# Latent attention: the low-rank rows of the first two pairs of query tiles are loaded ahead of the loads of w_out

## The chip, the cores and the metric

The kernel runs on one core of a Trainium2 chip. The metric is the device time of one launch in microseconds (us); times before are the median of three runs. One further execution was recorded by the hardware profiler, and all rows of the profile come from that one.

## The reference, cut to what matters

Two layers of a hybrid block over 1024 tokens with 1024 features. Each layer has a mixer (differential attention, latent attention and a state-space model side by side, concatenated and multiplied by `w_out`) and a squared-ReLU MLP. The part that the change touches is latent attention:

```python
def _mla(cq, ckv, kr, cos, sin, q_norm_g, w_uq, kv_norm_g, w_ukv):
    q = (_rmsnorm(cq, q_norm_g) @ w_uq).reshape(b, s, MLA_HEADS, MLA_NOPE + MLA_ROPE)
    qn = q[..., :MLA_NOPE]
    qr = _apply_rope(q[..., MLA_NOPE:], cos[:, :, None, :], sin[:, :, None, :])
    kv = (_rmsnorm(ckv, kv_norm_g) @ w_ukv).reshape(b, s, MLA_HEADS, MLA_NOPE + MLA_V)
    kn, v = kv[..., :MLA_NOPE], kv[..., MLA_NOPE:]
    kr = _apply_rope(kr, cos, sin)
    ...
        sc = (jnp.einsum('bqhd,bkhd->bhqk', qnb, kn)
              + jnp.einsum('bqhr,bkr->bhqk', qrb, kr)).astype(jnp.float32) * scale
        p = _masked_softmax(sc, _chunk_mask(start, s))
        return jnp.einsum('bhqk,bkhe->bqhe', p.astype(v.dtype), v)
```

`cq` (256 features) and `ckv` (128 features) are the low-rank rows: 384 floats for each token, projected from the layer's input. The mask lets a query see keys up to the end of its own chunk of 64 tokens, so query tile t needs the keys of tiles 0 to t.

## The kernel before

The 1024 tokens are 8 tiles of 128 (t = 0 to 7). Large products are done as three float32r products each (`mm3`, L191 to L193), from operands split into a high and a low part. The splitting costs a copy on ScalarE (ACT) and a subtraction on VectorE (DVE) for each operand. All DMAs are issued by SyncE (SP), whose queue is in order.

A layer's mixer is written as Python generators that emit instructions and are interleaved by `weave` (L1410): each stream has a weight, and the stream with the smallest progress emits next. The generators fix the source order; the framework's scheduler then fixes the order on each engine when the program is built, and it may put an instruction ahead of one that stands earlier in the source.

The streams that meet around the change, in `mixer`:

- `in_proj` (L749) projects the layer's input. It writes the low-rank rows and the rope part of the keys to a DRAM tensor `d_c` (L827, L828), and at its end runs the state-space model, tile by tile (`ssm`, L1173; its products are L1260, L1271 and L1282, its result is stored at L1289). At the mark "hidden" the last tile of it is still to come.
- `attention` (L1003) is the differential attention; each of its four heads ends with a store of its output into `d_cc` (L997).
- `mla` (L1099) is the latent attention. `lora` (L1019) loads its weights and returns three steps for a tile t. `first(t)` loads 384 floats for each token from `d_c` (L1046), scales them by the two root-mean-square factors (L1047, L1048, DVE), transposes them (L1051, PE) and copies them out (L1054, ACT). `second(t)` multiplies by `w_uq` (L1061) and `w_ukv` (L1063) and applies the rope. `third(t)` transposes queries and keys for all heads (L1090) and splits them (L1094, L1095).
- `load_wout` (L1294) loads eight tiles of `w_out` of 512 KB each (L1298) and splits them (L1302 and L1303, or L1305 on ACT and L1306 on DVE), for the out-projection (`out_proj`, L1311).

In `mla` the local function `ahead(n, i)` does the steps for query pair i, that is tiles 2i and 2i + 1. Pair 0 is done before the mark "hidden" (L1139 to L1142). Pair i + 1 is done between the heads of pair i (L1165): `first` of its first tile after head 0, `first` of its second tile and `second` of its first after head 1, `second` of its second after head 2. Pair i + 1 then begins with `third` (L1146) of both its tiles.

Three weaves follow one another (L1374 to L1378). The second ends when `attention` is done and `in_proj` and `mla` have both reached "hidden". The third weaves the rest of `in_proj`, query pair 0 of `mla`, and `load_wout`; so the loads of tiles 2 and 3 stand between those of `w_out` in the source. After it come the out-projection of tiles 0 and 1 beside query pair 1, and so on.

Buffers come from an arena of 17,856 words for each partition (`Arena`, L44). `get` takes, among the free places that fit, the one whose words were released longest ago; `put` releases. A load into a place must wait until whatever read or wrote the words before is done. Lookups for blocks of 256 words or more go in steps of 256 words.

Of the kernel before, what the change touches and what calls it, by code (L numbers as in the profile page):

```python
# [17 lines left out]
P = 128  # L18
# [12 lines left out]
WOW = 16  # L31
GROUPS = [2] + [4] * 6 + [2, 4]
LEAD = 6
C_Q, C_K, C_V, C_CQ, C_CKV, C_KR, C_Z, C_XBC, C_DT = 0, 256, 512, 768, 1024, 1152, 1184, 1696, 2464

SLOT = 2048
# [70 lines left out]
class Net:  # L107
# [125 lines left out]
    def mlp_up(self, l, hT, bg, late):  # L233
# [27 lines left out]
        N = FF // (2 * P)  # L261
        todo = [(i, True, False) for i in range(LEAD)] + [(i, i >= LEAD, True) for i in range(N)]
        staged = []
# [32 lines left out]
        stage()  # L296
        parts = self.chain(*(forms() for _ in range(LEAD + N)))
        queue = [next(parts) for _ in range(3)]
# [720 lines left out]
    def lora(self, l, st):  # L1019

        nc, F, I = self.nc, self.F, self.i
        p = st["p"]
        wuq, wukv = F.get(2, 384, top=True), F.get(512, top=True)
        nc.sync.dma_start(wuq, I["w_uq"][l].rearrange("(k p) n -> p k n", p=P))
        nc.sync.dma_start(wukv, I["w_ukv"][l])
        for k in range(2):
            nc.scalar.activation(wuq[:, k], wuq[:, k], AF.Copy, scale=p["uq"][k])
        nc.scalar.activation(wukv, wukv, AF.Copy, scale=p["ukv"])
        css = st["css"]
        nc.vector.tensor_add(css[:, 0], css[:, 0], css[:, 1])  # L1030
        rq = self.rsqrt(css[:, 0], 8, 1.0 / 256, RMS_EPS)
        rkv = self.rsqrt(css[:, 2], 8, 1.0 / 128, RMS_EPS)

        kr = F.get(8, 32, top=True)
        tmp = F.get(8, 32)
        k0 = F.get(8, 32)
        nc.sync.dma_start(k0, self.d_c[l].rearrange("(t p) c -> p t c", p=P)[:, :, 384:416])
        nc.vector.tensor_mul(kr.rearrange("p t (a f) -> p t a f", a=2), k0.rearrange("p t (a f) -> p t a f", a=2), self.rcos)
        for a in range(2):
            nc.vector.tensor_mul(tmp[:, :, a * 16:a * 16 + 16], k0[:, :, 16 - a * 16:32 - a * 16], self.rsin[:, :, a, :])  # L1040
        nc.vector.tensor_add(kr, kr, tmp)
        F.put(tmp, k0)

        def first(t):
            cn = F.get(384)
            nc.sync.dma_start(cn, self.d_c[l][t * P:t * P + P, 0:384])  # L1046
            nc.vector.tensor_scalar(cn[:, 0:256], cn[:, 0:256], rq[:, t:t + 1], None, op0=ALU.mult)  # L1047
            nc.vector.tensor_scalar(cn[:, 256:384], cn[:, 256:384], rkv[:, t:t + 1], None, op0=ALU.mult)  # L1048
            ps = self.bank("t")[:, 0:384]
            for k in range(3):  # L1050
                nc.tensor.transpose(ps[:, k * P:k * P + P], cn[:, k * P:k * P + P], self.ident)  # L1051
            F.put(cn)
            cT = F.get(384)
            nc.scalar.copy(cT, ps)  # L1054
            return cT

        def second(t, cT):
            pq = self.bank()[:, 0:384]
            for k in range(2):
                s = slice(k * P, k * P + P)  # L1060
                nc.tensor.matmul(pq, cT[:, s], wuq[:, k], start=k == 0, stop=k == 1)  # L1061
            pk = self.bank()
            nc.tensor.matmul(pk, cT[:, 256:384], wukv, start=True, stop=True)  # L1063
            F.put(cT)
            q = F.get(4, 96)
            pqv = pq.rearrange("p (h e) -> p h e", e=96)
            nc.vector.tensor_copy(q[:, :, 0:64], pqv[:, :, 0:64])
            tq = F.get(4, 32)
            cb = self.rcos[:, t].rearrange("p a f -> p (a f)").unsqueeze(1).to_broadcast([P, 4, 32])
            nc.vector.tensor_mul(q[:, :, 64:96], pqv[:, :, 64:96], cb)  # L1070
            for a in range(2):
                nc.vector.tensor_mul(tq[:, :, a * 16:a * 16 + 16], pqv[:, :, 80 - a * 16:96 - a * 16],
                                     self.rsin[:, t, a].unsqueeze(1).to_broadcast([P, 4, 16]))
            nc.gpsimd.tensor_add(q[:, :, 64:96], q[:, :, 64:96], tq)
            F.put(tq)
            kt = F.get(4, 96)
            pkv = pk.rearrange("p (h e) -> p h e", e=128)
            nc.scalar.copy(kt[:, :, 0:64], pkv[:, :, 0:64])
            nc.gpsimd.tensor_copy(kt[:, :, 64:96], kr[:, t].unsqueeze(1).to_broadcast([P, 4, 32]))
            assert st["heads"] >= (2 if t < 4 else 4)  # L1080
            nc.scalar.copy(st["vml"][:, t], pkv[:, :, 64:128])
            return q, kt

        def third(t, qk):
            tok = slice(t * P, t * P + P)
            dsts = st["QT"][t // 2 % 2][:, :, :, t % 2 * P:t % 2 * P + P], st["KT"][:, :, :, tok]
            pt = self.bank2()
            for n, src in enumerate(qk):
                for h in range(4):
                    nc.tensor.transpose(pt[0:96, (n * 4 + h) * P:(n * 4 + h + 1) * P], src[:, h], self.ident)  # L1090
                F.put(src)
            for n, dst in enumerate(dsts):
                pv = pt[0:96, n * 512:n * 512 + 512].rearrange("p (h q) -> p h q", q=P)
                nc.scalar.copy(dst[0:96, :, 0], pv)  # L1094
                nc.vector.tensor_sub(dst[0:96, :, 1], pv, f32(dst[0:96, :, 0]))  # L1095

        return first, second, third, lambda: F.put(kr, wuq, wukv)

    def mla(self, l, st, cc):  # L1099

        nc, F = self.nc, self.F
        first, second, third, done = self.lora(l, st)
        a, b = {}, {}

        def scores(h, i, pt):
            QT, KT = st["QT"][i % 2][:, h], st["KT"][:, h]
            ll, rl = self.sm(2, "ml_l"), self.sm(2, "ml_rl")
            for tt in range(2):
                n = P * (2 * i + tt + 1)
                tok = slice(tt * P, tt * P + P)  # L1110
                S = self.bank2()
                for c0 in range(0, n, 512):
                    c1 = min(n, c0 + 512)
                    self.mm3(S[:, c0:c1], QT[0:96, 0, tok], QT[0:96, 1, tok],
                             KT[0:96, 0, c0:c1], KT[0:96, 1, c0:c1], True, c1 < n)
                nc.tensor.matmul(S[:, n - 64:n], self.chunk[0:96, 0:P], self.chunk[0:96, P:192], start=False, stop=True)  # L1116
                p = F.get(n)
                self.softmax(S, n, p, self.sm(1, "nm"), ll[:, tt:tt + 1])
                pt.append(p)
                yield  # L1120
            nc.vector.reciprocal(rl, ll)
            pt.append(rl)

        def values(h, i, pt):
            rl = pt.pop()
            yield from self.p_times_v(pt[0], pt[1], i, st["vml"][:, :, h], rl, cc[i][:, :, 256 + h * 64:320 + h * 64])
            F.put(*pt)

        def ahead(n, i):
            t = 2 * i  # L1130
            if n == 0:
                a[t] = first(t)
            elif n == 1:
                a[t + 1] = first(t + 1)
                b[t] = second(t, a.pop(t))
            elif n == 2:
                b[t + 1] = second(t + 1, a.pop(t + 1))

        for n in range(3):  # L1139
            ahead(n, 0)  # L1140
            yield 2.0
        yield "hidden"  # L1142
        held, last = iter(()), None
        for i in range(4):
            for t in (2 * i, 2 * i + 1):
                third(t, b.pop(t))  # L1146
                yield 2.0
                next(held, None)
            cc[i] = F.get(2, D, top=True)
            rows = self.d_cc[l][i * 256:i * 256 + 256].rearrange("(t p) e -> p t e", p=P)  # L1150
            nc.sync.dma_start(cc[i][:, :, 0:256], rows[:, :, 0:256])
            nc.sync.dma_start(cc[i][:, :, 512:1024], rows[:, :, 512:1024])
            for h in range(4):
                pt = []
                for _ in scores(h, i, pt):
                    yield 2.0 + 2 * i
                    next(held, None)
                for _ in held:
                    yield 1.0
                if last is not None:  # L1160
                    yield last
                    last = None
                held = values(h, i, pt)
                if i < 3:
                    ahead(h, i + 1)  # L1165
            last = i
        done()
        for _ in held:
            yield 1.0
        yield last  # L1170
# [436 lines left out]
```

## Time and profile before

| what | us |
|---|---|
| median of 3 runs | 2797.93 |
| lowest and highest of the 3 | 2793.36, 2808.04 |
| the profiled execution's own time | 2798.41 |
| its span, from the first to the last instruction | 2796.6 |
| PE busy in the span | 2621.3 |
| DVE busy | 1749.1 |
| ACT busy | 1110.3 |
| POOL busy | 583.9 |

Times in the profile are counted from the start of the span. PE is TensorE, PEld its weight loads, POOL is GpSimd; a "q" behind an engine (SPq) is its sequencer, and the issue of a DMA is listed there with the time that the issue took, not the transfer. A row of a timeline has start, length, engine, source line, operation, what it writes and reads, and a count; in brackets stand the idle time of the engine before it and what ended that. Latent attention begins at about 447 us in layer 0 and 1810 us in layer 1; the out-projections begin at about 545 and 1896 us.

### The profile page before, as it was taken

Reading aid. Unit: us, or ns where it says so; the run is one execution under the profiler, and the core shown is the slowest. Engines: PE = TensorE matmul, PEld = TensorE weight load, DVE = VectorE, ACT = ScalarE, POOL = GpSimd, SP = SyncE. Lnnn points to the kernel's source line nnn. Section 1 sums busy time; section 2 is a strip of 40 time slices with the busy share of each in tenths; the row PEclk is TensorE's granted clock in tenths of the full one; section 3 lists DMA queues with packets and bytes.
Section 4 is the critical chain, followed back from the end, with each engine's and each line's share of the span. In section 5 each row is a group of like instructions: output and inputs, shape, how many; then the busy total and the mean of one; then the engine's idle time right before and its main releaser. Section 6 shows DMA issues by size and latency. Waiting matters only on the chain.

```text
span 2796.6 us, 34697 instructions
## 1 busy us (share of the span) xinstructions
PE 2621.3 (94%) x12530; PEld 2049.1 (73%) x12530; DVE 1749.1 (63%) x3223; ACT 1110.3 (40%) x2145; POOL 583.9 (21%) x517
## 2 busy tenths in 40 slices
PE   5799999799889999999999998989988999999998
PEld 3677776577667777777778776767766888788886
DVE  7767666544888877666585676664458645543435
ACT  5333334444544446121143434454454555521212
POOL 1341233310244230000021113341014422000002
PEclk9899979899999999999999998989999999999999
DMA  6441312321455557444331131132134432531313
GB/s 228 109 138 55 99 39 75 111 67 53 134 172 168 161 160 242 147 131 140 98 119 49 57 100 60 51 118 72 52 121 136 136 108 103 185 131 61 121 49 102
DMA packets 268527, 311.54 MB, mean 111 GB/s; under 512 B 28674, under 2 KB 212164, under 8 KB 268356
## 3 DMA queue, kind: packets, MB, share of 16 engines
q1 hardware_dynamic: 268356, 309.32, 34.5%
q8 instruction: 99, 1.62, 0.2%
q14 instruction: 72, 0.59, 0.1%
HBM read 242.85 MB, written 66.43 MB: 111 GB/s over the span
## 4 chain that ended last, share of the span: by engine, by line
PE 59%; DVE 5%; DMA 2%; ACT 2%; issue 1%; POOL 1%; DVEq 0%; SPq 0%; ACTq 0%; POOLq 0%
PE bank_b L191 9%; PE bank_b L193 9%; PE bank_b L192 9%; PE bank_s L191 8%; PE bank_s L192 8%; PE bank_s L193 8%; PE bank_s L967 1%; PE bank_a L914 1%; DVE split L231 1%; PE bank_t L927 1%; DVE arena_f L639 1%; PE bank_t L581 1%; PE bank_b L1260 1%; ACT split L230 0%; PE bank_a L943 0%
## 5 line engine op out<-in xcount | busy, mean ns | idle before, releaser
L191 PE MATMUL bank_b<-split 128*128 128x512 f32 (+2 forms) x1824 | 722.1, 396 | 30.5 <-DVE arena_f L217 11.5
L193 PE MATMUL bank_b<-split 128*128 128x512 f32 (+2 forms) x1824 | 702.9, 386 | 2.1 <-DVE split L231 1.3
L192 PE MATMUL bank_b<-split 128*128 128x512 f32 (+2 forms) x1824 | 702.4, 385 | 0.0
L230 ACT CAST split<-arena_f 128x512 fp32r<-128x512 f32 (+1 forms) x424 | 305.1, 749 | 701.4 <-PE bank_s L192 454.3
L191 PE MATMUL bank_s<-split 128*128 128x512 f32 (+2 forms) x1152 | 454.4, 397 | 24.8 <-ACT arena_f L902 6.9
L192 PE MATMUL bank_s<-split 128*128 128x512 f32 (+2 forms) x1152 | 450.9, 391 | 2.3 <-DVE split L231 1.8
L193 PE MATMUL bank_s<-split 128*128 128x512 f32 (+2 forms) x1152 | 448.3, 389 | 0.0
L231 DVE TENSOR_TENSOR split<-arena_f,split 128x512 fp32r<-128x512 f32 (+1 forms) x424 | 386.6, 931 | 94.6 <-ACT split L230 94.3
L191 PEld LDWEIGHTS bank_b<-split 128*128 128x128 f32 x1824 | 349.8, 192 | 108.7 <-ACT split L230 19.5
L193 PEld LDWEIGHTS bank_b<-split 128*128 128x128 f32 x1824 | 348.5, 191 | 69.5 <-issue 3.9
L192 PEld LDWEIGHTS bank_b<-split 128*128 128x128 f32 x1824 | 349.5, 192 | 64.3 <-issue 4.6
L408 DVE TENSOR_TENSOR arena_f<-arena_f,bank_s 128x1024 f32<-128x1024 f32 x126 | 153.6, 1219 | 241.3 <-PE bank_s L193 241.1
L191 PEld LDWEIGHTS bank_s<-split 128*128 128x128 f32 (+1 forms) x1152 | 218.0, 190 | 81.8 <-ACT arena_f L902 10.1
L192 PEld LDWEIGHTS bank_s<-split 128*128 128x128 f32 (+1 forms) x1152 | 219.2, 190 | 48.4 <-DVE split L231 3.5
L193 PEld LDWEIGHTS bank_s<-split 128*128 128x128 f32 (+1 forms) x1152 | 219.0, 190 | 44.6 <-issue 0.8
L901 DVE TENSOR_REDUCE nm<-bank_s 128x1 f32<-128x128 f32 (+3 forms) x192 | 141.0, 752 | 123.0 <-PE bank_s L1116 72.6
L902 ACT ACTIVATE arena_f<-bank_s,nm 128x128 f32<-128x128 f32 (+4 forms) x192 | 142.1, 742 | 163.6 <-DVE nm L901 119.7
L570 DVE SCALAR_TENSOR_TENSOR arena_f<-arena_f,cond 128x128 f32<-128x128 f32 x448 | 162.0, 388 | 46.4 <-DMA arena_f<-in_b_ada 20.4
L696 POOL TENSOR_TENSOR arena_f<-arena_f 128x1024 f32<-128x1024 f32 x14 | 33.6, 2400 | 462.2 <-ACT rstd_y L182 347.6
L930 ACT COPY arena_f<-bank_t 128x512 f32<-128x512 f32 (+1 forms) x160 | 86.9, 543 | 100.6 <-PE bank_t L927 93.4
L246 ACT ACTIVATE arena_f<-arena_f 128x512 f32<-128x512 f32 x128 | 81.0, 633 | 109.9 <-DVE arena_f L331 51.3
L967 PE MATMUL bank_s<-split 32*128 32x512 f32 (+3 forms) x576 | 117.1, 386 | 7.4 <-ACT arena_f L902 5.1
(281 smaller groups left out, 3189.5 us busy)
## 6 DMA issues: line engine op xcount, KB each, us to landing
arena_f<-in_w_ada SPq DMA_DIRECT2D x80, 512.0 KB
d_r<-arena_f SPq DMA_DIRECT2D x128, 256.0 KB
arena_f<-in_w_up SPq DMA_DIRECT2D x32, 1024.0 KB
arena_f<-d_r SPq DMA_DIRECT2D x64, 512.0 KB
arena_f<-in_w_down SPq DMA_DIRECT2D x64, 512.0 KB
arena_f<-d_x SPq DMA_DIRECT2D x36, 512.0 KB
d_x<-arena_f SPq DMA_DIRECT2D x23, 512.0 KB
arena_f<-in_w_in SPq DMA_DIRECT2D x20, 512.0 KB
```

The lines of the kernel that those rows point to most:

```text
L191: mm(out, wh, xh, start=start, stop=False)
L192: mm(out, wh, xl, start=False, stop=False)
L193: mm(out, wl, xh, start=False, stop=stop)
L230: self.nc.scalar.copy(hi, src)
L231: (eng or self.nc.vector).tensor_sub(lo, src, f32(hi))
L246: nc.scalar.activation(t, t, AF.Relu)
L408: nc.vector.tensor_add(y[t], y[t], ps)
L570: nc.vector.scalar_tensor_tensor(acc, in0=w[:, k], scalar=self.cond[:, k:k + 1], in1=acc, op0=ALU.mult, op1=ALU.add)
L901: nc.vector.tensor_reduce(nm, S[:, 0:n], axis=AX.X, op=ALU.max, negate=True)
L902: nc.scalar.activation(p[:, 0:n], S[:, 0:n], AF.Exp, bias=nm, accum_out=ls)
L930: nc.scalar.copy(held, ps[:, 0:w])
L967: nc.tensor.matmul(S[mp][:, c0:c1], Q[rw, a, tok], K[rw, b, c0:c1], start=a == b, stop=a == 1 and c1 < n)
```

## The change

The load is taken out of `first` into a function `load(t)` of its own, and `first` takes the loaded block. `mla` loads tiles 0 and 1 together at its start, and tiles 2 and 3 (`EARLY`) just before the mark "hidden"; tiles 4 to 7 are loaded where they were. `rows` now names the loaded blocks, so the view of `d_cc` is renamed `src`.

```diff
+EARLY = 2, 3
...
-        def first(t):
+        def load(t):
             cn = F.get(384)
             nc.sync.dma_start(cn, self.d_c[l][t * P:t * P + P, 0:384])
+            return cn
+
+        def first(t, cn):
             nc.vector.tensor_scalar(cn[:, 0:256], cn[:, 0:256], rq[:, t:t + 1], None, op0=ALU.mult)
...
-        return first, second, third, lambda: F.put(kr, wuq, wukv)
+        return load, first, second, third, lambda: F.put(kr, wuq, wukv)
...
-        first, second, third, done = self.lora(l, st)
+        load, first, second, third, done = self.lora(l, st)
         a, b = {}, {}
+        rows = {t: load(t) for t in (0, 1)}
...
+        def row(t):
+            return rows.pop(t) if t in rows else load(t)
+
         def ahead(n, i):
             t = 2 * i
             if n == 0:
-                a[t] = first(t)
+                a[t] = first(t, row(t))
             elif n == 1:
-                a[t + 1] = first(t + 1)
+                a[t + 1] = first(t + 1, row(t + 1))
                 b[t] = second(t, a.pop(t))
...
         for n in range(3):
             ahead(n, 0)
             yield 2.0
+
+        rows.update({t: load(t) for t in EARLY})
         yield "hidden"
```

More of the change, by code (lines that the diff above doesn't have):

```diff
@@ L1149, in mla @@
             cc[i] = F.get(2, D, top=True)
-            rows = self.d_cc[l][i * 256:i * 256 + 256].rearrange("(t p) e -> p t e", p=P)
-            nc.sync.dma_start(cc[i][:, :, 0:256], rows[:, :, 0:256])
-            nc.sync.dma_start(cc[i][:, :, 512:1024], rows[:, :, 512:1024])
+            src = self.d_cc[l][i * 256:i * 256 + 256].rearrange("(t p) e -> p t e", p=P)
+            nc.sync.dma_start(cc[i][:, :, 0:256], src[:, :, 0:256])
+            nc.sync.dma_start(cc[i][:, :, 512:1024], src[:, :, 512:1024])
             for h in range(4):
```

## The prediction

> **What bounds the kernel now.** I read the page's first part, then the windows view, then PE's waits in the two stretches that the change touches, and last the timelines of PE, DVE, SP and ACT there.
>
> ```profile
> span 2796.6 us, 34697 instructions
> ## 1 busy us (share of the span) xinstructions
> PE 2621.3 (94%) x12530; PEld 2049.1 (73%) x12530; DVE 1749.1 (63%) x3223; ACT 1110.3 (40%) x2145; POOL 583.9 (21%) x517
> ```
>
> TensorE is busy for 94% of the span, so a change gains only where PE stands idle or is granted a slow clock. The change touches the end of the SSM part and the start of latent attention, once in each layer. The windows view (length, busy time of PE, PEld, DVE, ACT and POOL, granted clock, DMA share, GB/s) has these stretches:
>
> ```profile
> 500.00:515.00 15.00, 12.37 (x81) 9.16 (x79) 10.26 (x15) 10.03 (x20) 10.73 (x7) 1.00 0.71 230
> 515.00:545.00 30.00, 18.98 (x85) 12.65 (x85) 15.77 (x61) 14.18 (x39) 8.27 (x12) 0.66 0.30 93
> 1860.00:1872.00 12.00, 10.62 (x70) 7.45 (x67) 9.23 (x16) 8.68 (x17) 7.21 (x4) 1.00 0.60 186
> 1872.00:1900.00 28.00, 19.22 (x87) 13.52 (x87) 17.08 (x58) 15.74 (x41) 11.25 (x13) 0.70 0.51 167
> ```
>
> From 515 to 545 us (layer 0) PE idles 30.00 - 18.98 = 11.0 us, from 1872 to 1900 us (layer 1) 28.00 - 19.22 = 8.8 us, and the clock granted there is 0.66 and 0.70. The in-projection is over, the out-projection has not begun, and only the chains of latent attention are left. PE's waits, total, times and longest, first those of 440 to 560 us, then of 1810 to 1930:
>
> ```profile
> PE bank_t L1051 <- DVE arena_f L1047: 7.3, 1, 7.3
> ...
> PE bank_s L191 <- ACT arena_f L902: 3.9, 2, 2.8
> ...
> PE bank_t L927 <- ACT arena_f L1054: 1.7, 1, 1.7
> ```
>
> One wait stands out: 7.3 us in layer 0, before the transposes (L1051) of low-rank rows. The timelines of DVE, PE and SP say why:
>
> ```profile
> 531.28 0.35 DVE L1047 TENSOR_SCALAR arena_f<-arena_f,rs_y 128x256 f32<-128x256 f32 x1 [3.85 <-DMA arena_f<-d_c]
> ...
> 531.69 0.90 PE L1051 MATMUL bank_t<-ident,arena_f 128*128 128x128 f32 x3 [7.27 <-DVE arena_f L1047]
> ...
> 487.51 0.33 SPq L1298 DMA_DIRECT2D arena_f<-in_w_out  x1
> ...
> 497.79 0.33 SPq L1298 DMA_DIRECT2D arena_f<-in_w_out  x1
> ...
> 525.44 0.38 SPq L997 DMA_DIRECT2D d_cc<-arena_f  x1
> 528.03 0.37 SPq L1151 DMA_DIRECT2D arena_f<-d_cc  x1
> 528.45 4.51 SPq L1046 DMA_DIRECT2D arena_f<-d_c  x2
> ```
>
> It is the fourth group of L1051, so the rows are those of tile 3. Their load went out at 528.45, behind the store of the last differential head (525.44) and a load (528.03) that waits for that store. The DMA itself was short: the multiply began at 531.28, 2.8 us after the issue. So the row is late in SP's queue, not slow behind w_out's bytes. In the source the load stands between w_out loads; the change puts it ahead of all of them.
>
> **The change part by part.** Nothing is added or removed: 16 loads, 16 pairs of multiplies and all products stay. Moved are, in each layer, the load of tile 1 (to beside tile 0's) and of tiles 2 and 3 (to before the mark "hidden"), and with them the time for which three blocks of 384 words are held.
>
> Tile 1: PE has no wait on L1047 but the one above, so an earlier landing earns nothing; I take 0. If the held block pushes another load back it costs, and that is rival C.
>
> Tiles 2 and 3, layer 0. The 7.27 us of waiting go, since rows issued near 490 us (where w_out's first load goes out now) have landed long before 524. Next in PE's order behind L1051 stand the transposes of the probabilities of query pair 0, and ACT had finished their softmax:
>
> ```profile
> 523.86 0.47 ACT L902 ACTIVATE arena_f<-bank_s,nm 128x256 f32<-128x256 f32 x1 [1.52 <-DVE nm L901]
> ...
> 533.16 0.90 PE L927 MATMUL bank_t<-ident,arena_f 128*128 128x128 f32 x3 [0.57 <-ACT arena_f L1054]
> ```
>
> So nothing else is late there, and I count all of it, -7.3. Beside it the clock. These are the same groups of products of two tiles, before and after the wait:
>
> ```profile
> 497.39 1.46 PE L1061 MATMUL bank_b<-arena_f 128*128 128x384 f32 x4
> ...
> 499.85 1.02 PE L1063 MATMUL bank_b<-arena_f 128*128 128x512 f32 x2
> ...
> 533.86 2.77 PE L1061 MATMUL bank_b<-arena_f 128*128 128x384 f32 x4
> ...
> 536.42 1.87 PE L1063 MATMUL bank_b<-arena_f 128*128 128x512 f32 x2
> ```
>
> They took 4.64 us in place of 2.48, so 2.2 us are lost to the clock. With rows early they run in the full-clock stretch before 515 us, where PE has 15.00 - 12.37 = 2.6 us free. That stretch will not hold all of it, and the rest of the stage stays thinly filled; I take half, -1.1. Layer 0: -8.4, between -2 (another releaser takes over at once: ACT's softmax) and -13 (7.3 + 2.2 and a third of the 11.0 idle).
>
> The Trainium skill, "TensorE: Matmul & The Clock Gate", section on the HAM clock gate, has the array at half rate after an idle stretch until about 3.4 us of activity have passed. By that rule one cold start costs 1.7 us, and the layer's sum would be -9.0; the two groups above agree with the half rate (4.64 against 2.48), not with so short a ramp, since they are still slow 6 us after 531.69.
>
> Layer 1. Here the fourth row load is issued earlier, and the wait has another owner; SP, ACT and PE:
>
> ```profile
> 1869.88 0.33 SPq L1046 DMA_DIRECT2D arena_f<-d_c  x1
> ...
> 1877.58 1.15 ACT L1305 ACTIVATE split<-arena_f,cols 128x1024 fp32r<-128x1024 f32 x1 [2.32 <-DMA arena_f<-in_w_out]
> 1878.64 0.46 ACT L1054 COPY arena_f<-bank_t 128x384 f32<-128x384 f32 x1
> ...
> 1875.85 0.90 PE L1051 MATMUL bank_t<-ident,arena_f 128*128 128x128 f32 x3
> ...
> 1879.15 0.90 PE L927 MATMUL bank_t<-ident,arena_f 128*128 128x128 f32 x3 [1.71 <-ACT arena_f L1054]
> 1879.85 2.77 PE L1061 MATMUL bank_b<-arena_f 128*128 128x384 f32 x4
> 1882.41 1.30 PE L1063 MATMUL bank_b<-arena_f 128*128 128x512 f32 x2
> ```
>
> PE waits 1.71 us for the copy L1054, and that copy stands on ACT behind a w_out cast which waits for its DMA. Early rows take the copy out of this place, but the cast still holds ACT, and softmax is behind it; I count the wait at 0 (bounds 0 and -1.7). What goes is the slow clock of tile 3's products: 2.77 + 1.30 against 2.48, -1.6. Layer 1: -1.6, between -6 (two thirds of the 8.8 idle) and +4 (ACT's waits for w_out, 6.5 us in rival B's row, grow by more than half).
>
> Where the words come from. The arena hands out the words that were released longest ago. At "hidden" in layer 0 those are a block that w_out's first load takes now; the two row blocks will lie in it, and w_out's eight loads each move one place down. From the first two issues that is 497.79 - 487.51 = 10.3 us. What hides it:
>
> ```profile
> 521.91 1.28 DVE L1306 SCALAR_TENSOR_TENSOR split<-arena_f,cols,split 128x1024 fp32r<-128x1024 f32 x1
> ...
> 1899.05 1.28 DVE L1306 SCALAR_TENSOR_TENSOR split<-arena_f,cols,split 128x1024 fp32r<-128x1024 f32 x1 [1.66 <-ACT split L1305]
> ...
> 552.00 0.47 PE L191 MATMUL bank_b<-split 128*128 128x512 f32 x1
> ...
> 1907.64 0.48 PE L191 MATMUL bank_b<-split 128*128 128x512 f32 x1
> ```
>
> The last cast of w_out ends at 523.2 and the first product with it starts at 552.0 in layer 0, a cover of 29 us; in layer 1 it is 1900.3 and 1907.6, a cover of 7 us, and the first product uses the first tile of w_out, not the last. I take 0; if the cover is gone, up to 10.3 - 7.3 = 3 us in layer 1.
>
> After the stage all later blocks of the arena lie elsewhere, and waits for their words change. No row shows that; by PE's idle time after 560 us, 2237.00 - 2134.60 = 102 us, a tenth either way is 10 us. I take 0.
>
> ```profile
> 560.00:2797.00 2237.00, 2134.60 (x10105) 1683.40 (x10103) 1374.22 (x2447) 879.84 (x1626) 409.66 (x351) 0.97 0.35 113
> ```
>
> Sum: -8.4 - 1.6 = -10.0. The profiled execution took 2798.4 us (its span and 1.8 us around it), 0.5 us above the median of 2797.93, so the forecast is 2798.4 - 10.0 = **2788.4 us**.
>
> **Rivals.** A, more than that: with tiles 2 and 3 through their products by 515 us, both thin stretches close up. Their slow-clock share is 18.98 x 0.34 + 19.22 x 0.30 = 12.2 us, the idle 19.8. Half of these 32 gone is -16: 2782. For it: 7.3 us in one piece. Against it: most waits left are ACT's and DVE's own chain.
>
> B, slower: **SP blocked at the early loads, ACT blocked at w_out's casts.** Waits first of SP and of ACT in layer 0, then of ACT in layer 1:
>
> ```profile
> SPq L1298 <- PE bank_b L1260: 10.4, 2, 8.1
> ...
> ACT split L1305 <- DMA arena_f<-in_w_out: 3.6, 2, 2.3
> ...
> ACT split L1305 <- DMA arena_f<-in_w_out: 6.5, 4, 3.3
> ```
>
> SP stood 8.1 us for the words of w_out's first load; the early rows inherit that place, and w_out and the SSM's stores queue behind. If w_out's casts come 10.3 us later and softmax waits behind them on ACT, each layer loses up to 10.3 us; 20.6 less three quarters of the gain, 7.5, is +13: 2811. It decides once w_out's last cast in layer 0 ends after 552 - 10.3 = 542 us or ACT's waits for in_w_out exceed some 15 us a layer. Against it: the cover above. The Trainium skill, "DMA: Bandwidth & Descriptors", section on the anatomy of one DMA, says that a semaphore wait happens on the issuing sequencer before dispatch; by that rule the early loads hold back everything behind them, and the sum would be this rival's, 2811. The 8.1 us row agrees that SP waits so; whether PE pays, no row shows.
>
> C, nothing: the row is early, but PE waits as long for ACT's softmax or the SSM's last loads, which the block held for tile 1 delays. The layers' upper bounds, -2 and +4, make +2 or less: about 2798.
>
> **How the numbers follow.** Forecast 0.40, A 0.24, C 0.24, B 0.12. A change of 0.5% (14 us) is about what a measurement of this kernel can tell from none: faster means below 2784, slower above 2812. Faster: A and a little of the forecast's own range (2781 to 2795), 0.29; slower: most of B and a share of C's, 0.11; same 0.60. The range leaves out A's far end and B's: 2775 to 2806.
>
> **What would show it.** Right: four SP issues of L1046 before the first of L1298 in each layer; no PE wait on L1047; the fourth group of L1051 before 515 us; the first out-projection product some 8 us earlier in layer 0 (near 544) and about 2 in layer 1, net of layer 0's gain. Wrong: the wait reappears at L927, L967 or L191 with ACT as releaser (C), w_out's last cast later than 542 us (B), or a difference that arises after 700 us, where nothing of the change runs but the words lie elsewhere.

## The result: slower by 0.7%, and the time is lost far from the change

| | before | after |
|---|---|---|
| median of 8 runs each, us | 2797.65 | 2820.26 |
| lowest and highest | 2792.90, 2808.04 | 2812.10, 2829.46 |
| profiled execution | 2798.41 | 2812.10 |

The ratio of after to before is 1.0073, with a 95% interval of 1.0058 to 1.0088. The forecast was 2788.4 us, in a range of 2775 to 2806. Here and below a ratio compares with the kernel before on the same chip, whose median lies between 2797.65 and 2805.71 us by chip; it is estimated from all runs and is no quotient of two medians (2820.26 by 2797.65 is 1.0081).

Lines of the changed kernel are counted one higher than before up to the change, four higher behind `load` (L1051 is now L1055, L1061 is L1065) and ten higher behind `mla` (L1298 is now L1308). In the kernels with words of their own, further down, L1047 is L1055, L1051 is L1059, L1061 is L1069, L1235 is L1249 and L1298 is L1312.

First the change's own place. SP's timeline of after:

```profile
446.61 0.79 SPq L1047 DMA_DIRECT2D arena_f<-d_c  x2
...
481.84 0.32 SPq L1047 DMA_DIRECT2D arena_f<-d_c  x1
494.73 0.32 SPq L1047 DMA_DIRECT2D arena_f<-d_c  x1
505.73 4.70 SPq L1308 DMA_DIRECT2D arena_f<-in_w_out  x3
...
530.79 0.46 SPq L1308 DMA_DIRECT2D arena_f<-in_w_out  x1
```

The four row loads of layer 0 now go out ahead of w_out's first load, as the source says. But w_out's loads also moved: from 487.51 for the first one to 505.73, which is 18.2 us and not 10.3. PE's waits of after from 440 to 560 us (total, times, longest):

```profile
PE bank_t L928 <- ACT arena_f L1058: 5.7, 1, 5.7
PE bank_s L968 <- ACT arena_f L903: 3.6, 1, 3.6
PE bank_b L192 <- DVE arena_f L1293: 3.6, 1, 3.6
PE bank_s L192 <- DVE split L1099: 3.1, 1, 3.1
```

The wait of 7.3 us for the scaled rows is gone. In its place stands one of 5.7 us for the copy L1058. ACT's and PE's timelines of after say what held that copy:

```profile
528.37 1.15 ACT L1315 ACTIVATE split<-arena_f,cols 128x1024 fp32r<-128x1024 f32 x1 [1.43 <-DMA arena_f<-in_w_out]
529.64 1.04 ACT L1312 CAST split<-arena_f 128x1024 fp32r<-128x1024 f32 x1
530.60 0.57 ACT L1098 CAST split<-bank_s 96x512 fp32r<-96x512 f32 x1
531.07 0.47 ACT L1058 COPY arena_f<-bank_t 128x384 f32<-128x384 f32 x1
...
531.60 0.90 PE L928 MATMUL bank_t<-ident,arena_f 128*128 128x128 f32 x3 [5.73 <-ACT arena_f L1058]
```

In ACT's order the copy stands behind two casts of w_out: ACT waited 1.43 us for a tile of it, cast two in 1.15 and 1.04 us, and came to the copy at 531.07. That is what rival B described. So the thin stretch is as thin as before, in the windows view of after (length, PE, PEld, DVE, ACT, POOL, clock, DMA share, GB/s):

```profile
500.00:515.00 15.00, 13.17 (x80) 8.84 (x78) 9.29 (x20) 8.46 (x16) 4.80 (x4) 1.00 0.43 136
515.00:545.00 30.00, 18.75 (x95) 12.88 (x95) 19.76 (x54) 16.97 (x44) 15.51 (x16) 0.77 0.52 168
```

PE idles 11.3 us of the 30, against 11.0 before. The first product with w_out starts at 552.13 us, against 552.00.

One window of before bears on the clock, from which the prediction took part of its gain. It ends where the wait of 7.27 us begins:

```profile
517.00:524.00 7.00, 5.43 (x23) 4.78 (x24) 6.28 (x27) 5.09 (x16) 0.67 (x2) 0.55 0.26 90
```

The granted clock is 0.55 there, and no PE wait in it is longer than 0.75 us. So the clock had fallen before the wait, and the wait did not bring the fall.

Second, where the rest went. For each PE instruction of the kernel before I took the same one (same source line, same count) in the trace of after, and the difference of the two starts. Its median over 20 us is +3.5 us at 725 us, +18.2 at 1270, +15.0 at 1990 and +13.8 at the end. So as much as the whole loss between the two profiles arises in the MLP of layer 0, some 200 us behind the change. The profiled execution of after was its fastest run: the two profiles differ by 13.7 us, the medians by 22.6, and no trace shows where the rest arises. PE's waits from 720 to 1300 us and SP's from 740 to 860 us, of before:

```profile
PE bank_b L191 <- DVE arena_f L217: 11.5, 1, 11.5
...
SPq L270 <- DVE split L231: 7.1, 5, 2.8
```

and of after:

```profile
PE bank_b L192 <- ACT split L231: 16.0, 2, 8.4
PE bank_b L192 <- DVE arena_f L332: 3.4, 3, 1.6
PE bank_b L192 <- DVE arena_f L328: 2.3, 2, 1.6
...
SPq L271 <- DVE split L232: 20.7, 4, 10.0
```

L271 loads a part of `w_up` into arena words; L231 and L232, a helper, split such a part. SP stands 20.7 us in place of 7.1 until a split is done, as if a block of `w_up` now got words of one that is still in use. What PE's two long waits go back to stand in the timelines of SP, POOL, ACT and PE of after:

```profile
809.75 0.38 SPq L271 DMA_DIRECT2D arena_f<-in_w_up  x1
...
789.83 1.31 POOL L285 TENSOR_TENSOR arena_f<-arena_f 128x512 f32<-128x512 f32 x1 [11.48 <-DMA arena_f<-in_w_up]
...
786.25 2.70 ACT L231 CAST split<-arena_f 128x512 fp32r<-128x512 f32 x5 [2.70 <-DMA arena_f<-in_w_up]
...
802.19 0.62 ACT L231 CAST split<-arena_f 128x512 fp32r<-128x512 f32 x1 [2.96 <-POOL arena_f L286]
...
786.92 0.80 PE L192 MATMUL bank_b<-split 128*128 128x512 f32 x1 [7.62 <-ACT split L231]
802.86 0.80 PE L192 MATMUL bank_b<-split 128*128 128x512 f32 x1 [8.38 <-ACT split L231]
```

The Trainium skill, "DMA: Bandwidth & Descriptors", section on the anatomy of one DMA, puts a semaphore wait on the issuing sequencer, ahead of dispatch. The longest of SP's waits for a split, 10.0 us up to the issue at 809.75, agrees.

That PE pays for this wait is not shown, since both of its long waits end before 809.75. The first ends with a cast that waited for a `w_up` DMA. The second ends with a cast that waited for POOL, and POOL had begun its sums of `w_up` parts (L285, in before L284) at 789.83, when a `w_up` DMA landed. In before they begin at 784.73, and what they wait for is not a DMA:

```profile
784.73 1.69 POOL L284 TENSOR_TENSOR arena_f<-arena_f 128x512 f32<-128x512 f32 x1 [6.59 <-DVE arena_f L318]
```

So in after a part of `w_up` comes late. These two waits are not the whole loss: before has one of 11.5 us in the same place, and by the differences of starts 7.3 of the 14.7 us have arisen at 860 us, the rest behind it.

### The profile page after: what moved, and what is told of

The parts are those of the page before. It is cut to its first block, busy times and chain, and to the rows that moved or that the text cites. A ratio compares the mean times of both kernels' runs of the same rounds, so it can differ in the third digit from the quotient of the medians.

```text
span 2810.4 us, 34709 instructions
## 1 busy us (share of the span) xinstructions
PE 2632.8 (94%) x12530; PEld 2059.7 (73%) x12530; DVE 1746.1 (62%) x3223; ACT 1112.8 (40%) x2145; POOL 584.9 (21%) x517
## 5 line engine op out<-in xcount | busy, mean ns | idle before, releaser
L231 ACT CAST split<-arena_f 128x512 fp32r<-128x512 f32 (+1 forms) x424 | 306.0, 748 | 708.2 <-PE bank_s L193 426.2
L232 DVE TENSOR_TENSOR split<-arena_f,split 128x512 fp32r<-128x512 f32 (+1 forms) x424 | 387.8, 933 | 89.4 <-ACT split L231 88.6
L968 PE MATMUL bank_s<-split 32*128 32x512 f32 (+3 forms) x576 | 118.8, 387 | 10.9 <-ACT arena_f L903 8.4
```

What stands on the lines that cost most here:

```text
L231: self.nc.scalar.copy(hi, src)
L232: (eng or self.nc.vector).tensor_sub(lo, src, f32(hi))
L968: nc.tensor.matmul(S[mp][:, c0:c1], Q[rw, a, tok], K[rw, b, c0:c1], start=a == b, stop=a == 1 and c1 < n)
```

## The experiments

Theory A: the early loads do what they should, but holding three blocks of 384 words at other times makes the arena deal other words to every later block, and the order that the program is built with follows the new dependencies; that costs the time, in layer 0's MLP above all. Theory B: the early loads themselves cost it, through SP's queue and ACT's casts. An edit stands against the changed kernel where nothing else is said.

**Loads early, places as before.** The rows of tiles 1 to 3 go into words that the arena does not deal, the dead part of the differential heads' values `vda` (tiles 1 and 2 share a place, one after the other); the arena is asked for 384 words and gets them back where the kernel before did that.

```diff
+        flat = st["vda"].rearrange("p a b c -> p (a b c)")
+        own = {n: flat[:, w:w + 384] for n, w in ((1, 512), (2, 512), (3, 1024))}
         def load(t):
-            cn = F.get(384)
+            cn = own[t] if t in own else F.get(384)
...
         def first(t, cn):
+            held = F.get(384) if t in own else cn
...
-            F.put(cn)
+            F.put(held)
```

> The loads of tiles 1, 2 and 3 go out early as in the change, but into words of the differential values that are dead by then; the arena's blocks are taken and released at the old points, so that every other block lies where it lay before. Theory A (what costs is that the arena re-deals the words of all later blocks, and the order built on them): the 16 us that the changed kernel loses in layer 0's MLP are gone, 2788 to 2802 us. Theory B (the early loads cost by themselves, w_out's casts come later and hold ACT before softmax): they are early here too, so 2810 us or more.

Measured: 2788.45 us, ratio 0.9968 (0.9956 to 0.9980): faster than both kernels. The two groups of products of tile 3, which took 4.64 us in before and were to come ahead of 515 us, stand here in its trace:

```profile
514.25 2.77 PE L1069 MATMUL bank_b<-arena_f 128*128 128x384 f32 x4
...
516.81 1.91 PE L1071 MATMUL bank_b<-arena_f 128*128 128x512 f32 x2
```

They come earlier and are as slow as before, 4.68 us.

**Places early, loads as before.** The counterpart: `load` only takes the block, and the DMA goes out at the head of `first`.

```diff
         def load(t):
-            cn = F.get(384)
-            nc.sync.dma_start(cn, self.d_c[l][t * P:t * P + P, 0:384])
-            return cn
+            return F.get(384)
         def first(t, cn):
+            nc.sync.dma_start(cn, self.d_c[l][t * P:t * P + P, 0:384])
```

> The blocks for tiles 1, 2 and 3 are taken from the arena at the change's early points, but each load is issued only where it was issued before. A: the words are dealt as in the changed kernel, so the loss comes back without any early load, 2810 to 2826 us, with most of it between 780 and 1280 us of the span. B: no load is early, 2794 to 2802 us.

Measured: 2816.66 us, ratio 1.0060 (1.0037 to 1.0083), nearly all that the change costs, without one early load. The four cases are about 2799 (neither), 2788 (loads), 2817 (places) and 2820 (both).

**One tile early, through the arena**, so that only tile 1's load moves:

```diff
-EARLY = 2, 3
+EARLY = ()
```

> Only tile 1's load is early; tiles 2 and 3 are loaded where they were before. A: the words after 447 us are dealt in a third way, so a third time, anywhere from 2788 to 2822 us, and not the same as before's. B: nothing stands ahead of w_out's loads that did not before, 2794 to 2802 us.

Measured: 2827.54 us, ratio 1.0098 (1.0066 to 1.0130), above even the range of theory A. The smallest part of the change costs the most; what is lost does not grow with what is loaded early.

**No change but the deal.** The kernel before takes 384 words from the arena and gives them back at once ahead of each MLP. No instruction is added.

```diff
+            F.put(F.get(384))
             with self.phase(t=1, b=3):
                 self.mlp_up(l, hT, bg, late)
```

> The kernel before, with a block of 384 words taken from the arena and released at once at the start of each MLP: no instruction is added or moved in the source, only the ages of 384 words differ. A: the words of the MLP's blocks are dealt anew and the time moves by 3 us or more, either way. If the dealing does not matter: 2794 to 2802 us.

Measured: 2823.73 us, ratio 1.0085 (1.0057 to 1.0113). Taking and returning a block costs as much as the whole change. Three variants place it: ahead of layer 0's MLP only, of layer 1's only, and with 1024 words in both.

> The kernel before, with 384 words taken from the arena and given back at once ahead of layer 0's MLP alone; no instruction is added. Theory A (the words dealt to the MLP of layer 0 cost the time): the kernel with this edit in both layers lost 22 us between 740 and 1280 us, and this one has the same deal there; it ends at 2815 to 2828 us, slower than before by 0.6 to 1.0%, and the MLP of layer 0 again shows PE waits of some 15 us for the parts of w_up. Rival (the loss is spread over both layers, or is not tied to the first MLP): at most half of it, 2800 to 2811 us.

> The same take and return ahead of layer 1's MLP alone. Everything up to that MLP (some 2160 us) is as in the kernel before. Theory A: nothing is lost before 2160 us; the kernel with the edit in both layers came back by some 7 us after it, so 2788 to 2798 us. Rival (each take costs, wherever it stands): 2808 to 2815 us.

> The kernel before, with 1024 words in place of 384 taken and given back ahead of each MLP. Theory A says only that the deal decides: the time moves by some tenths of a per cent to either side, 2785 to 2830 us, and the change begins behind 740 us. Rival (the loss belongs to a shift of 384 words and to nothing else): as before, within 0.15%.

Measured: layer 0 only 2826.69, ratio 1.0079 (1.0062 to 1.0095); layer 1 only 2798.50 beside 2805.71 for the kernel before on that chip, ratio 0.9973 (0.9955 to 0.9991); 1024 words 2818.17, ratio 1.0050 (1.0032 to 1.0069). The loss sits in layer 0's MLP; the same take in layer 1 gains a little. The windows view, SP's waits from 740 to 860 us and PE's timeline for the take in layer 0 alone:

```profile
720.00:1300.00 580.00, 545.00 (x2367) 425.14 (x2366) 427.48 (x811) 227.24 (x376) 118.74 (x120) 0.98 0.49 155
...
SPq L270 <- DVE split L231: 27.4, 7, 8.2
...
803.14 0.80 PE L191 MATMUL bank_b<-split 128*128 128x512 f32 x1 [13.32 <-ACT split L230]
```

Beside it the windows of before, and of after:

```profile
720.00:1300.00 580.00, 561.66 (x2467) 442.94 (x2467) 444.70 (x825) 236.83 (x382) 117.78 (x123) 0.99 0.49 159
```

```profile
720.00:1300.00 580.00, 550.59 (x2398) 432.30 (x2397) 429.24 (x811) 229.41 (x373) 115.01 (x122) 0.98 0.50 158
```

PE idles 580.00 - 561.66 = 18.3 us before, 29.4 after and 35.0 here, and SP's wait for the splits is 7.1, 20.7 and 27.4 us. The same two views of all kernels part them in two: those that deal this MLP the words of before have 18.3 to 20.5 us of idle PE and 6.6 to 8.3 us of that wait, those that deal others 25.8 to 35.0 and 9.6 to 27.5. They do not go in step within the second group: one tile early has 31.1 with 13.2, the take of 1024 words 25.8 with 9.6.

**Which tile brings the gain of early loads?** With own words, first tile 3 alone:

```diff
-EARLY = 2, 3
+EARLY = 3,
...
+        own = {3: flat[:, 1024:1408]}
...
-        rows = {t: load(t) for t in (0, 1)}
+        rows = {0: load(0)}
```

Then tiles 1 and 2 alone:

```diff
-EARLY = 2, 3
+EARLY = 2,
...
+        own = {n: flat[:, 512:896] for n in (1, 2)}
```

The rest of the edit is that of the first experiment.

> Only tile 3's rows are loaded ahead of w_out, into words of its own that the arena does not hand out; tiles 1 and 2 are loaded where the kernel before loads them, and all blocks of the arena are dealt as before. The prediction's mechanism (tile 3's late rows cost layer 0 its 7.27 us wait and the slow clock behind it): the whole gain of the kernel with three own loads, 2786 to 2792 us. Rival (the order of the small steps around, tiles 1 and 2 among them, brings it): 2794 to 2799 us.

> The counterpart: tiles 1 and 2 have early loads into words of their own, tile 3 is loaded where the kernel before loads it. The prediction's mechanism: PE's wait for tile 3's rows in layer 0 stays (7 us), and the time is that of before, 2795 to 2800 us. Rival: most of the gain comes here, 2787 to 2792 us.

Neither came as the prediction's mechanism has it. Tile 3 alone: 2808.84 beside 2801.26, ratio 1.0013 (0.9993 to 1.0034), no gain, and above what the rival said too. Tiles 1 and 2 alone: 2786.79, ratio 0.9955 (0.9942 to 0.9969), the whole gain. Yet the wait behaved as expected: with tile 3 early, PE's longest wait for scaled rows from 440 to 560 us is the first row here, and with tiles 1 and 2 the second:

```profile
PE bank_t L1059 <- DVE arena_f L1055: 1.2, 1, 1.2
```

```profile
PE bank_t L1059 <- DVE arena_f L1055: 7.2, 1, 7.2
```

The gain of tiles 1 and 2 arises elsewhere: their trace runs 3.0 us behind that of before at 1670 us and 6.3 ahead of it at 1790, in the state-space part of layer 1. There the kernel before has this wait, from 1700 to 1770 us:

```profile
PE bank_t L1235 <- ACT arena_f L930: 8.1, 1, 8.1
```

With tiles 1 and 2 early no PE wait above 0.2 us is left there. The instructions are the same, but they stand in another order: DVE, ACT and PE differ there from the kernel before in about a dozen places. With tile 3 alone the order differs at 713, 1466 and 1705 us, and by the differences of starts its trace loses 6, 3 and 8 us there, more than the 6.5 that it gains where the row load moved.

**Does early loading bring that order?** Two last kernels: own early rows in layer 0 alone, and a mixed one with tiles 1 to 3 in layer 0 and tiles 1 and 2 in layer 1, where the order around 1740 us is again that of before.

Against the kernel with three own loads, first the one, then the other:

```diff
-        own = {n: flat[:, w:w + 384] for n, w in ((1, 512), (2, 512), (3, 1024))}
+        own = {n: flat[:, w:w + 384] for n, w in ((1, 512), (2, 512), (3, 1024)) if l == 0}
...
-        own = {n: flat[:, w:w + 384] for n, w in ((1, 512), (2, 512), (3, 1024))}
+        own = {n: flat[:, w:w + 384] for n, w in ((1, 512), (2, 512), (3, 1024)) if l == 0 or n < 3}
```

The early loads are cut in the same way; the other tiles of layer 1 load where the kernel before does.

> The kernel with own words for the early rows of tiles 1, 2 and 3, but in layer 0 alone; in layer 1 the loads stand where the kernel before has them. Theory (the gain of early rows is layer 0's wait for tile 3; layer 1's term is about nothing): 2786 to 2791 us, as with both layers. Rival (layer 1's early rows bring part of it): 2793 to 2798 us.

> Own words for tiles 1, 2 and 3 in layer 0, and for tiles 1 and 2 alone in layer 1. The kernel with early tiles 1 and 2 in both layers was faster by 0.45%; its trace lacks a PE wait of 8.1 us at 1748 us, in layer 1's state-space part, and keeps the 7.2 us wait for tile 3's rows in layer 0. Theory (that gain came from another built order around 1740 us, which early rows of layer 1 do not bring by themselves; here the order there is again that of before): the 8 us wait is back, and the time is that of the kernel with three own loads, 2785 to 2792 us. Rival (early rows of tiles 1 and 2 in layer 1 bring it, and it adds to layer 0's gain): 2774 to 2782 us.

Measured: the mixed one 2788.60 us, ratio 0.9949 (0.9931 to 0.9967), and its wait from 1700 to 1770 us is back:

```profile
PE bank_t L1249 <- ACT arena_f L931: 8.1, 1, 8.1
```

So the early rows of tiles 1 and 2 do not add to layer 0's gain; the order did. Layer 0 alone: 2782.84, ratio 0.9926 (0.9907 to 0.9945), the fastest of all, and below what was expected. PE's waits from 440 to 560 us, SP's and PE's timelines and the windows view of this kernel:

```profile
PE bank_b L1069 <- DVE arena_f L885: 2.6, 1, 2.6
PE bank_a L915 <- ACT arena_f L931: 2.2, 1, 2.2
...
486.57 0.32 SPq L1050 DMA_DIRECT2D arena_f<-d_c  x1
491.68 0.33 SPq L1312 DMA_DIRECT2D arena_f<-in_w_out  x1
...
515.83 3.11 SPq L1312 DMA_DIRECT2D arena_f<-in_w_out  x2
...
542.39 0.47 PE L192 MATMUL bank_b<-split 128*128 128x512 f32 x1
...
515.00:545.00 30.00, 25.73 (x138) 18.54 (x138) 23.03 (x70) 20.72 (x55) 13.65 (x16) 0.89 0.44 137
```

Here w_out's loads stand where they were (first issue 491.68, 4 us later than before in a trace that runs 4 us late at this point), PE waits for no copy of rows, PE idles 4.3 us of the 30 instead of 11.0, and the first out-projection product starts at 542.39 instead of 552.00.

**All kernels by stretch.** The difference of starts to the kernel before, as above: how much it grows (+, time lost) in a stretch, in us. Other stretches are left out; the last column has all from 495 us on.

| kernel | 495 to 570 (latent attention, layer 0) | 725 to 1270 (MLP) | 1670 to 1790 (state space) | 1790 to 1990 (latent attention, layer 1) | 495 to the end |
|---|---|---|---|---|---|
| after | +0.9 | +14.7 | -3.2 | +2.1 | +12.7 |
| own words, tiles 1 to 3 | -12.0 | +1.9 | +1.4 | +0.4 | -0.7 |
| own words, layer 0 alone | -12.9 | +3.6 | +1.4 | -3.7 | -9.7 |
| own words, mixed | -11.4 | +3.0 | -0.2 | -3.9 | -11.6 |
| own words, tile 3 | -6.5 | +1.4 | +8.1 | -0.3 | +12.6 |
| own words, tiles 1, 2 | -1.8 | +3.6 | -9.3 | +0.4 | -4.1 |
| places alone | +1.6 | +15.4 | -5.3 | +2.0 | +11.8 |
| one tile early | +4.1 | +17.1 | +15.9 with the next | | +27.2 |
| take ahead of both MLPs | +0.3 | +22.0 | +3.9 | +9.7 | +22.1 |
| take in layer 0 | 0.0 | +23.3 | +2.5 | +6.9 | +22.4 |
| take in layer 1 | +0.1 | +2.2 | -0.2 | -0.5 | -3.0 |
| take of 1024 words | 0.0 | +10.9 | -6.8 | +7.7 | +15.7 |

The second column parts the kernels in two: those that deal layer 0's MLP the words of before lose 1.4 to 3.6 us there, those that deal others 10.9 to 23.3. The first column shows what early rows are worth while the words stay: -11.4 to -12.9 with tiles 1 to 3, half of it with tile 3 alone. The third shows, in the kernels with own words, the built order, with no row load anywhere near. The last column and the medians agree in sign and not in size: the three own loads gain 12 us in their stretch and end at -0.7 in the trace, while the medians of that kernel and of before differ by 10.9 us. Single executions of one kernel lie up to 30 us apart (before on one chip, 2794.58 to 2824.34), so a trace settles a stretch and not a total.

## Why the prediction was wrong, step by step

- **"So the row is late in SP's queue", and -8.4 for layer 0:** the mechanism was right, the size too small. With the words kept, the wait goes and the stretch gains 11.4 to 12.9 us, close to the upper bound of 13 that was set. Tile 3's wait is about half of it; the rest comes only when tiles 1 and 2 are early too.
- **The clock, -1.1:** this term came about in another way than it was worked out. The products of tile 3 do not run at full clock: they take 4.68 us with own words in both layers and 2.34 + 1.02 = 3.36 with layer 0 alone, against 4.64 before and 2.48 at full clock. Nor had the wait brought the slow clock, which was 0.55 ahead of it. What rose is the clock of the whole stretch, from 0.66 to 0.89 between 515 and 545 us with layer 0 alone. The first out-projection product, put near 544, comes at 542.39 there; that says little, since it comes at 543.41 in a kernel that differs from before only behind it.
- **"w_out's eight loads each move one place down ... I take 0":** this step failed. The cover was measured to the first product with w_out, 29 us, and the last of the eight loads, issued at 530.79, was still in time for that (552.13). What was late was ACT's copy of the rows, queued behind the casts: PE waited 5.73 us for it, and the stretch gained nothing (+0.9). It was rival B's mechanism; own words, which leave w_out's loads in place, have -12.0 there. How much of this difference of 12.9 us is ACT's doing, and how much that of the other words and order, no run shows; with the places alone and no load early the stretch gains nothing either (+1.6). B's deciding point (a last cast behind 542 us) was wrong, since the blocking began earlier.
- **"After the stage all later blocks of the arena lie elsewhere ... I take 0":** this is the step that failed most. Its bound of 10 us either way was too narrow as well: the MLP of layer 0 alone costs 14.7 us in after and 23.3 with a bare take of 384 words. That a difference would arise behind 700 us, where nothing of the change runs, had been named as the sign of it.
- **Layer 1, -1.6:** no gain shows. The stretch moves by +2.1 us in after and by +0.4 with own words; it moves by -3.7 where layer 1 loads as before and by -3.9 in the mixed kernel, where tiles 1 and 2 are early. So moves of 4 us come with early rows and without, and -1.6 is too small to be told from them. Whether early rows in layer 1 cost something stays open: 0.9926 without them stands against 0.9968 with three of them, but on another chip, and against 0.9949 with two on the same chip, where the intervals overlap.
- **The sum:** with the words kept, -10.0 comes close to the measured -9.0 us (ratio 0.9968) and -11 (the medians), but with luck: layer 0's term was too small, layer 1's brought nothing that shows, and other stretches, through the built order, moved by as much as either. The kernel with layer 0 alone has -20.7 by its ratio. The change as made gains nothing in layer 0's stretch and loses 15 us in the MLP.

What is shown: places without loads cost the time, and loads without places gain it. A take without a load, ahead of layer 0's MLP alone, costs as much, so the deal of the arena's words is the cause. What is only read from the traces: that the MLP loses through `w_up` loads waiting for words in use. The deal changes the built order too, on PE from 741 us on in the kernel with the take in layer 0, and no kernel has the new words with the old order, or separate words for `w_up`; so how much is waiting for words and how much is order stays open.

## What to carry to other kernels

Where one allocator serves a whole program, a block held a little longer or earlier deals other words to everything behind it, and a scheduler may build another order; ask for both before a gain of some 10 us is trusted, and give a moved transfer words of its own so that the rest stays. To learn what a re-deal is worth, take and return a block and change nothing else: here that alone moved the time by up to 0.85%. Judge an edit by the stretch that it touches as well as by the total, and count as cover not the consumer of a transfer alone but whatever is queued behind the cast that waits for it.

## What the hardware showed unasked

The clock fell without idle time, and not in every execution. Up to 680 us the kernel before and the one with a take ahead of both MLPs have the same instructions in the same order on every engine. Their windows (before first, then the other kernel):

```profile
340.00:400.00 60.00, 59.78 (x267) 43.41 (x266) 38.82 (x85) 23.71 (x55) 21.17 (x16) 0.80 0.14 47
360.00:380.00 20.00, 20.00 (x66) 14.06 (x64) 13.25 (x26) 6.29 (x16) 6.35 (x5) 0.52 0.08 23
```

```profile
360.00:380.00 20.00, 20.00 (x109) 15.24 (x108) 17.46 (x34) 7.55 (x18) 9.02 (x6) 1.00 0.19 55
...
543.41 0.48 PE L191 MATMUL bank_b<-split 128*128 128x512 f32 x1
```

PE is busy for all 20 us in both, at a granted clock of 0.52 and of 1.00; in the first it idles 60.00 - 59.78 = 0.2 us from 340 to 400 us. The first out-projection product comes at 552.00 and 543.41, 8.6 us apart with nothing changed ahead of it. The Trainium skill, "TensorE: Matmul & The Clock Gate", section on the HAM clock gate, has the array fall back to half rate after an idle window of about 3.4 us; PE showed no such gap here (idle 0.2 us), and the measurement decides. The table by stretch therefore starts at 495 us, where kernels with equal order stay within 0.3 us of one another.
